# Transposing q and k of the dilated stage by crossbar transfers instead of by TensorE

## The chip, the cores and the metric

The kernel runs on one core of a Trainium2 chip. The metric is the device time of one execution in microseconds (us). A core has a matrix engine (TensorE, PE in the profile, with PEld for its weight loads), a vector engine (DVE), a scalar engine (ACT), GpSimd (POOL) and SyncE (SP), which in this kernel issues most of the transfers; 16 DMA engines carry them. Each engine runs its own instructions strictly in the order in which they stand, and waits on semaphores where it needs another engine's result. SP does the same with the transfers that it issues: a transfer that must wait for its data holds back every transfer behind it.

## The reference

A two-layer encoder over 1024 tokens of width 1024, in float32. Layer 0 mixes tokens by latent attention, layer 1 by dilated sliding-window attention; each layer ends with a squared-ReLU MLP. The change concerns layer 1's mixer alone:

```python
def dilated_mixer(h, pos, w_in, g_q, g_k, rel_bias, w_o):
    proj = (h @ w_in).reshape(B, S, N_DIL_GROUPS, 3, DIL_HEADS, DIL_HEAD_DIM)
    for gi, (window, dilation) in enumerate(DIL_GROUPS):   # (128,1) (512,4) (2048,16)
        q = rms_norm(proj[:, :, gi, 0], g_q[gi])
        k = rms_norm(proj[:, :, gi, 1], g_k[gi])
        v = proj[:, :, gi, 2]
        o, lse = dilated_group(q, k, v, pos, table, window, dilation)
        ...
    # the three groups' outputs are merged by the softmax of their log denominators, then @ w_o
```

There are 16 heads of 64 in each of 3 groups. A query sees 128 keys around it (in the dilated order), with a bias by relative position.

## The kernel before, in words

Products of float32 accuracy are made of float16: a matrix is split into a high half `hi` = f16(x) and a low half `lo` = f16(x - hi), and three matmuls (hi·hi, lo·hi, hi·lo) are summed in PSUM. This is the helper `mm3` (L532 to L534), and `products` (L2345) does the same for the scores. The program holds a second, float32r form of everything (`half` is False), which runs only if a check on the data fails; it does not run here.

The dilated stage is the method `dil`. It takes 3 groups × 8 pairs of heads × 4 token-tile pairs = 96 **steps**; a step is (group g, head pair `pr`, `tp`), where `tp` counts pairs of 128-token tiles. A head pair's four steps form a *unit*. The loop over steps is software pipelined; one pass of the loop emits, in this order:

- `attend` (L2381): for two token tiles whose q and k are ready: 12 score matmuls (`products`, out `pss`), then `scores` (bias and maximum on DVE, L2366; exponentials on ACT, L2372), then the probabilities' halves `ph` (high half on ACT, L2409; low half on DVE and POOL, L2410), then one crossbar transpose issued on SP, `pT<-ph` (L2411).
- The projection of this step's q and k: 48 matmuls of 128×256 into `psproj`, in two halves of 24 (`project`).
- Between the two halves: `stacks` of the step before the last one: four float32 transposes on PE against the identity, `psq<-ident,qn` (L2316), then the split into halves while PSUM is read: high half on ACT (L2321, scaled by 64), low half on DVE (L2322). Both write the tile `kT`, which holds for one unit, in f16, k transposed for all 1024 tokens and **two slots** of q (256 columns each, by `tp % 2`).
- `av` (L2424, L2425): the product with V of the attention emitted one pass earlier, from `pT`.
- `qkstep` of this step's projection: squares on ACT (L2295), sum on DVE (L2296), reciprocal root (ACT L132, L133; DVE L134 to L136), a guard sum on POOL (L2300 to L2302), then `qn` = normalised q and k in the tokens' layout (DVE L2305), and q's gain on POOL (L2307).

So what `qkstep` makes in pass n is transposed in pass n+2 and used by `attend` in pass n+3; an `attend` of pass n is used by `av` in pass n+1. Inside these bounds a scheduler orders each engine's instructions when the program is built.

SP issues for a unit four `wqkr` weight loads (L1968), one bias tile `bt` (L2354), the finished `U` of a unit (L2448 in group 0, two of L2452 in group 1, none in group 2), and for every second unit the V tiles `vraw` (four transfers in group 0, seven in group 1, four in group 2; L2250 to L2266), beside one `pT` for each step. Each transfer takes the next of eight completion semaphores in turn.

Of the kernel before, what the change touches and what calls it, by code (L numbers as in the profile page):

```python
# [20 lines left out]
P = 128  # L21
D = 1024
S = 1024
# [18 lines left out]
class K:  # L42
# [2148 lines left out]
    def dil(self, at0, at1, tail, wqk, vd):  # L2191


        nc, a, tc = self.nc, self.a, self.tc
# [5 lines left out]
        D_ = lambda name, shape, dt, bufs: dpool.tile(list(shape), dt, tag=name, bufs=bufs, name=self.nm(name))  # L2200
# [6 lines left out]
        if self.half:  # L2207
            most = dpool.tile([P, 8], F32, name="most", bufs=1)
            nc.gpsimd.memset(most, 0.0)
            self.nseen += 1  # L2210
            s_ = self.seen[:, self.nseen - 1 : self.nseen]
            nc.vector.tensor_reduce(s_, gain, op=ALU.max, axis=AX.XY, apply_absolute_value=True)
            nc.vector.tensor_scalar(s_, s_, 4.0, None, op0=ALU.mult)
        else:
            nc.vector.tensor_scalar(gain, gain, self.ss, None, op0=ALU.mult)
        stat = dpool.tile([P, 3, 8, 2, H], F32, name="stat", bufs=1)
        Ud = self.DR([8, S, 2, P], "U")
        oTd = self.DR([6, 2, P, 2, 512], "oTd", F16 if self.half else F32)
# [70 lines left out]
        def qkstep(u, tp, ps):  # L2289

            g = u["g"]
            p8 = ps.rearrange("p (n e) -> p n e", e=64)
# [4 lines left out]
            r = self.rstd(ms, 8, "dr", self.half)  # L2297
# [4 lines left out]
                nc.gpsimd.tensor_tensor(most, most, y4, op=ALU.add)  # L2302
            qn = self.T("qn")
            q8 = qn.rearrange("p (n e) -> p n e", e=64)
            nc.vector.tensor_tensor(q8, p8, r.unsqueeze(2).broadcast_to([P, 8, 64]), op=ALU.mult)  # L2305
            qq = qn.rearrange("p (i n e) -> p i n e", i=2, e=64)[:, :, 0:2, :]
            nc.gpsimd.tensor_tensor(qq, qq, gain[:, g : g + 1, :].unsqueeze(1).broadcast_to([P, 2, 2, 64]), op=ALU.mult)  # L2307
            return qn

        def stacks(u, tp, qn):  # L2310

            ps = PS("psq")
            for k in range(2):
                for i in range(2):
                    c = i * 256 + (1 - k) * P
                    nc.tensor.transpose(ps[:, (2 * k + i) * P : (2 * k + i + 1) * P], qn[:, c : c + P], self.ident)  # L2316
            s1 = 4 + tp % 2
            hi, lo = (u["k"][:, k, :].rearrange("p (s x) -> p s x", x=256)[:, tp : s1 + 1 : s1 - tp, :] for k in range(2))
            x = ps.rearrange("p (k x) -> p k x", k=2)
            if self.half:  # L2320
                nc.scalar.activation(hi, x, AF.Copy, scale=64.0)  # L2321
                nc.vector.scalar_tensor_tensor(lo, x, 64.0, hi, op0=ALU.mult, op1=ALU.subtract)  # L2322
            else:
                nc.scalar.activation(hi, x, AF.Copy)
                nc.vector.tensor_tensor(lo, x, hi.bitcast(F32), op=ALU.subtract)
            for i in range(2):
                c = S + (tp % 2 * 2 + i) * P
                u["q"][2 * tp + i] = u["k"][:, :, c : c + P]

        def span(g, t):  # L2330
# [214 lines left out]
        end = max(n for n, x in enumerate(steps) if x is not None)  # L2545
# [75 lines left out]
        for n, step in enumerate(steps):  # L2621
# [271 lines left out]
```

## Time and profile before

| | |
|---|---|
| time, 3 runs | 3007.86 us median (3006.16 to 3011.14) |
| the profiled execution's own time | 3005.26 us |
| its span | 3003.1 us, granted TensorE clock 0.985 |
| busy over the span | PE 94%, DVE 75%, ACT 56%, POOL 31% |
| dilated stage, first to last score matmul | 1552 to 2321 us |
| PE busy in that stage | 710.58 us of 768.5 us |
| largest waits of PE there | on `pT` 25.0 us, on `kT` 14.8 us (DVE's half) and 7.8 us (ACT's half) |

The profile's page gives busy time by engine, 40 equal slices of the span, the transfers by queue, the chain that ended last, and the costliest groups of instructions. A group's row reads: line, engine, operation, output<-input, partitions × elements and type, count, then busy time or durations. In a timeline a row is start (us), duration (us), engine or queue, line, operation; `x2` at the end means that two such instructions in a row were merged, and their duration then runs from the first's start to the last's end, a wait between them included. "SPq" is SP's queue: its duration is the time for which SP was occupied with issuing, not the time of the transfer itself. A wait row reads: who waited, for whose result, total us, times, longest us.

### The profile page before, as it was taken

The numbers are of one execution on the slowest core, as the hardware profiler recorded it, in microseconds if no ns is written. First come the engines' busy times: TensorE is split into PE (matmuls) and PEld (weight loads), VectorE is DVE, ScalarE is ACT, GpSimd is POOL, SyncE is SP. The second block draws the span as 40 slices with busy tenths as digits, with TensorE's granted clock in tenths as the row PEclk, the third lists the DMA queues.
The fourth block names the chain that finished last, engine by engine and source line by source line (L and its number), as shares of the span: only waits on it lengthen the run. The fifth ranks groups of instructions, "written<-read, shape, count | busy, mean of one in ns | idle before, by whom it ended". The sixth has DMA issues, their size and how long they took to land. (4 is left out here: it accounts for less than half of the span.)

```text
span 3003.1 us, 54490 instructions
## 1 busy us (share of the span) xinstructions
PE 2827.4 (94%) x20148; PEld 1676.0 (56%) x20148; DVE 2251.4 (75%) x4902; ACT 1684.2 (56%) x3491; POOL 922.6 (31%) x1276
## 2 busy tenths in 40 slices
PE   6878999999999999999999989998998989999998
PEld 5634566544444444444468878876875434444443
DVE  5687777658988966788768877776886699779565
ACT  4677888825455534533238777775664355555341
POOL 6578888700211000000123344453552002110010
PEclk9999999999999999999999999999999999999999
DMA  6267455425654799546436666565656555457763
GB/s 209 72 169 161 94 117 101 131 84 188 235 188 168 251 278 289 199 159 225 171 116 148 146 139 165 145 128 117 150 129 171 144 191 210 158 186 248 238 196 86
DMA packets 589680, 503.08 MB, mean 168 GB/s; under 512 B 292277, under 2 KB 482018, under 8 KB 589402
## 3 DMA queue, kind: packets, MB, share of 16 engines
q1 hardware_dynamic: 553722, 400.74, 47.9%
q0 software_dynamic: 25248, 87.22, 7.9%
q10 hardware_dynamic: 10432, 11.54, 1.6%
q8 instruction: 159, 2.61, 0.4%
q14 instruction: 119, 0.97, 0.1%
HBM read 317.40 MB, written 125.12 MB: 147 GB/s over the span
## 5 line engine op out<-in xcount | busy, mean ns | idle before, releaser
L534 PE MATMUL psm<-hf,wf 128*128 128x512 f16 x896 | 335.8, 381 | 11.1 <-DVE wf L161 11.1
L532 PE MATMUL psm<-hf,wf 128*128 128x512 f16 x896 | 341.0, 381 | 5.0 <-ACT wf L156 5.0
L533 PE MATMUL psm<-d,d 128*128 128x512 f16 x896 | 340.8, 381 | 4.7 <-DVE d L161 4.7
L534 PE MATMUL psm<-d,d 128*128 128x512 f16 x896 | 340.7, 380 | 0.0
L533 PE MATMUL psm<-hf,wf 128*128 128x512 f16 x896 | 340.6, 380 | 0.0
L532 PE MATMUL psm<-d,d 128*128 128x512 f16 x896 | 335.0, 380 | 0.3 <-ACT d L156 0.3
L1276 POOL TENSOR_TENSOR pp<-p,pp 128x1024 f16<-128x1024 f32 x125 | 275.4, 2209 | 57.9 <-ACT pp L1269 47.8
L532 PE MATMUL psproj<-wqk,hTp 128*128 128x256 f16 x1024 | 283.0, 276 | 0.0
L533 PE MATMUL psproj<-wqk,hTp 128*128 128x256 f16 x1024 | 282.3, 276 | 0.0
L534 PE MATMUL psproj<-wqk,hTp 128*128 128x256 f16 x1024 | 282.0, 275 | 0.0
L156 ACT ACTIVATE d<-ufr 128x1024 f16<-128x1024 f32 x112 | 117.8, 1052 | 211.3 <-PE psm L534 173.3
L897 DVE TENSOR_REDUCE mx<-pmx 128x1 f32<-128x512 f32 x240 | 162.8, 687 | 78.8 <-PE pmx L895 77.4
L161 DVE SCALAR_TENSOR_TENSOR d<-ufr,d 128x1024 f16<-128x1024 f32 x112 | 136.5, 1219 | 76.5 <-ACT d L156 76.4
L1268 ACT ACTIVATE p<-pss 128x512 f32<-128x512 f32 x256 | 149.9, 590 | 43.2 <-PE pss L1259 41.8
L2372 ACT ACTIVATE pd<-pd,dnb 128x192 f32<-128x192 f32 (+2 forms) x384 | 167.3, 437 | 4.1 <-POOL y L2301 2.3
L534 PEld LDWEIGHTS <-wf 128*128 128x128 f16 x896 | 87.8, 98 | 123.3 <-DVE wf L161 19.2
L532 PEld LDWEIGHTS <-wf 128*128 128x128 f16 x896 | 87.9, 98 | 112.9 <-ACT wf L156 10.9
L534 PEld LDWEIGHTS <-d 128*128 128x128 f16 x896 | 87.9, 98 | 111.0 <-issue 6.4
L532 PEld LDWEIGHTS <-d 128*128 128x128 f16 x896 | 88.0, 98 | 106.3 <-issue 2.2
L533 PEld LDWEIGHTS <-d 128*128 128x128 f16 x896 | 87.9, 98 | 106.4 <-issue 2.5
L2410 POOL TENSOR_TENSOR ph<-pd,ph 128x512 f16<-128x512 f32 (+1 forms) x121 | 113.3, 942 | 109.3 <-ACT ph L2409 109.1
L533 PEld LDWEIGHTS <-wf 128*128 128x128 f16 x896 | 88.0, 98 | 104.9 <-issue 1.8
(439 smaller groups left out, 8122.2 us busy)
## 6 DMA issues: line engine op xcount, KB each, us to landing
ufr<-uf SPq DMA_DIRECT2D x112, 512.0 KB
w2r<-in_mlp_w SPq DMA_DIRECT2D x96, 512.0 KB
adaw<-in_ada_w SPq DMA_DIRECT2D x80, 512.0 KB
w1r<-in_mlp_w SPq DMA_DIRECT2D x64, 512.0 KB
wqkr<-in_dil_w_in SPq DMA_DIRECT2D x96, 256.0 KB
wvr<-in_dil_w_in SPq DMA_DIRECT2D x34, 512.0 KB
uf<-ub POOLq DMA_DIRECT2D x32, 512.0 KB, 3.8
uf<-ua POOLq DMA_DIRECT2D x32, 512.0 KB, 3.3
```

The source lines that it names most:

```text
L156: nc.scalar.activation(hi, src, AF.Copy, scale=scale)
L161: return nc.vector.scalar_tensor_tensor(lo, src, scale, hi, op0=ALU.mult, op1=ALU.subtract, accum_out=self.seen[:, self.nseen - 1 : self.n ...
L532: mm(out, lh, rh, start=first, stop=False)
L533: mm(out, lh, rl, start=False, stop=False)
L534: mm(out, ll, rh, start=False, stop=last)
L897: nc.vector.tensor_reduce(maxes[h][:, 2 * j + b : 2 * j + b + 1], ps, op=ALU.max, axis=AX.X)
L1268: nc.scalar.activation(p[:, b * 512 : (b + 1) * 512], ps[b], AF.Exp, scale=1.0 / self.ss)
L1276: eng.tensor_tensor(q[:, 1], p, q[:, 0], op=ALU.subtract)
L2372: nc.scalar.activation(p[:, e, lo:hi], p[:, e, lo:hi], AF.Exp, scale=1.0 / self.ss, bias=nb[:, e : e + 1], accum_out=stat[:, g, t, 1, 2 * ...
L2410: (nc.gpsimd if i or u["g"] == 2 else nc.vector).tensor_tensor(lo, p, hi, op=ALU.subtract)
```

## The change

In the f16 form, q and k are no longer transposed by PE and split out of PSUM. `qkstep`'s last DVE instruction now also multiplies by 64. A new function `qkturn`, called one pass after `qkstep` (so one pass earlier than the transposes of before), splits `qn` in the tokens' layout into a float16 tile `hl`: high half on ACT, low half on POOL, each 128×512. Then four crossbar transposes on SP (`dma_start_transpose`) put `hl`'s high k, high q, low k and low q, each 128 tokens × 256 columns, transposed into `kT`. `kT` has three slots for q instead of two. `stacks` then has nothing to do for these steps and only hands the slots on; the last two of the 96 steps still go by PE.

```diff
+        NQ = 3 if self.half else 2
...
-            nc.vector.tensor_tensor(q8, p8, r.unsqueeze(2).broadcast_to([P, 8, 64]), op=ALU.mult)
+            rb = r.unsqueeze(2).broadcast_to([P, 8, 64])
+            if self.half:
+                nc.vector.scalar_tensor_tensor(q8, p8, 64.0, rb, op0=ALU.mult, op1=ALU.mult)
+            else:
+                nc.vector.tensor_tensor(q8, p8, rb, op=ALU.mult)
...
+        def qkturn(u, tp, qn):
+
+            hl = D_("hl", (P, 2, 2, 2, P), F16, 2)
+            x = qn.rearrange("p (i s c) -> p s i c", i=2, s=2)
+            nc.scalar.activation(hl[:, 0], x, AF.Copy)
+            nc.gpsimd.tensor_tensor(hl[:, 1], x, hl[:, 0], op=ALU.subtract)
+            for k in range(2):
+                for s, c in ((1, tp * 256), (0, S + tp % NQ * 256)):
+                    nc.sync.dma_start_transpose(out=u["k"][:, k, c : c + 256].rearrange("p (i c) -> p i c", c=P),
+                                                in_=hl[:, k, s].rearrange("p i c -> p (i c)"))
+            for i in range(2):
+                c = S + (tp % NQ * 2 + i) * P
+                u["q"][2 * tp + i] = u["k"][:, :, c : c + P]
+
         def stacks(u, tp, qn):
 
+            if qn is None:
+                return
             ps = PS("psq")
...
-            if self.half:
-                nc.scalar.activation(hi, x, AF.Copy, scale=64.0)
-                nc.vector.scalar_tensor_tensor(lo, x, 64.0, hi, op0=ALU.mult, op1=ALU.subtract)
-            else:
-                nc.scalar.activation(hi, x, AF.Copy)
-                nc.vector.tensor_tensor(lo, x, hi.bitcast(F32), op=ALU.subtract)
+            nc.scalar.activation(hi, x, AF.Copy)
+            nc.vector.tensor_tensor(lo, x, hi if self.half else hi.bitcast(F32), op=ALU.subtract)
...
-                                      "k": D_("kT", (P, 2, S + 512), self.DT, 2), "U": self.G("U", (P, 8, P), F32)}
+                                      "k": D_("kT", (P, 2, S + 256 * NQ), self.DT, 2), "U": self.G("U", (P, 8, P), F32)}
...
+            if self.half and stacking is not None and n < end:
+                qkturn(*stacking)
+                stacking = stacking[:2] + (None,)
             stk.append(stacking)
```

How the instructions move. On PE, at the middle of one step's projection in group 1 (`hTp` is the permuted input's half, `wqk` the weights), there stood before:

```order
L533 MATMUL psproj_22794<-wqk_22612,hTp_20623 128x256
L534 LDWEIGHTS hTp_20623
L534 MATMUL psproj_22794<-wqk_22612,hTp_20623 128x256
L2316 MATMUL psq_22819<-ident,qn_22603 128x128 x4
L532 LDWEIGHTS hTp_20201
L532 MATMUL psproj_22794<-wqk_22609,hTp_20201 128x256
```

and there stands now:

```order
L533 MATMUL psproj_22801<-wqk_22619,hTp_20630 128x256
L534 LDWEIGHTS hTp_20630
L534 MATMUL psproj_22801<-wqk_22619,hTp_20630 128x256
L532 LDWEIGHTS hTp_20208
L532 MATMUL psproj_22801<-wqk_22616,hTp_20208 128x256
```

The four transposes are gone and the two halves of the projection follow each other; the rest of PE's order in a step is as it was.

On SP, late in group 1, over two units with a set of V loads; before:

```order
L2354 DMA bt_23873<-bias_138 128x2x256
L2411 DMA_TRANSPOSE pT_23185<-ph_23184 128x16x128
L2452 DMA U<-U_22198 512x1x128
L2411 DMA_TRANSPOSE pT_23335<-ph_23334 128x16x128
L2452 DMA U<-U_22198 512x1x128
L1968 DMA wqkr_23492<-in_dil_w_in 128x4x128 x2
L2411 DMA_TRANSPOSE pT_23470<-ph_23469 128x16x128
L2411 DMA_TRANSPOSE pT_23607<-ph_23606 128x16x128
L1968 DMA wqkr_23771<-in_dil_w_in 128x4x128 x2
```

and now, at the same place:

```order
L2428 DMA_TRANSPOSE pT_23342<-ph_23341 128x16x128
L1968 DMA wqkr_23214<-in_dil_w_in 128x4x128
L2323 DMA_TRANSPOSE kT_22759<-hl_23390 128x2x128 x4
L2469 DMA U<-U_22205 512x1x128 x2
L2428 DMA_TRANSPOSE pT_23477<-ph_23476 128x16x128
L1968 DMA wqkr_23499<-in_dil_w_in 128x4x128
L2323 DMA_TRANSPOSE kT_23323<-hl_23526 128x2x128 x4
L2428 DMA_TRANSPOSE pT_23614<-ph_23613 128x16x128
L1968 DMA wqkr_23499<-in_dil_w_in 128x4x128
L2323 DMA_TRANSPOSE kT_23323<-hl_23662 128x2x128 x4
L1968 DMA wqkr_23778<-in_dil_w_in 128x4x128
```

From one `pT` (128×16×128) to the next there now stand, nearly everywhere, four `kT` transposes of 128×2×128 (L2323) in the same queue.

On POOL, two steps' pieces of the same group; now:

```order
L2312 TENSOR_TENSOR qn_22610<-qn_22610,dgain 128x2x128
L2427 TENSOR_TENSOR ph_22636<-pd_22648,ph_22636 128x512
L2320 TENSOR_TENSOR hl_22686<-qn_22610,hl_22686 128x512
L2393 MEMSET pd_22789 128x2x64
L2395 MEMSET pd_22917 128x2x64
L2301 TENSOR_TENSOR y_3627_22749<-dry_22741 128x8
L2302 TENSOR_TENSOR y_3627_22749<-y_3627_22749 128x8
L2303 TENSOR_TENSOR most<-most,y_3627_22749 128x8
L2312 TENSOR_TENSOR qn_22753<-qn_22753,dgain 128x2x128
L2427 TENSOR_TENSOR ph_22777<-pd_22789,ph_22777 128x512
L2320 TENSOR_TENSOR hl_22826<-qn_22753,hl_22826 128x512
```

`hl`'s low half (L2320) is new; it stands mostly behind the low half of `ph` (L2427, L2410 before), which `pT` waits for. Otherwise POOL's order is that of before. On ACT `hl`'s high half (L2319) stands about where `kT<-psq` (L2321) stood.

More of the change, by code (lines that the diff above doesn't have):

```diff
@@ L2316, in stacks @@
                     nc.tensor.transpose(ps[:, (2 * k + i) * P : (2 * k + i + 1) * P], qn[:, c : c + P], self.ident)
-            s1 = 4 + tp % 2
+            s1 = 4 + tp % NQ
             hi, lo = (u["k"][:, k, :].rearrange("p (s x) -> p s x", x=256)[:, tp : s1 + 1 : s1 - tp, :] for k in range(2))
             x = ps.rearrange("p (k x) -> p k x", k=2)
-            if self.half:
-                nc.scalar.activation(hi, x, AF.Copy, scale=64.0)
-                nc.vector.scalar_tensor_tensor(lo, x, 64.0, hi, op0=ALU.mult, op1=ALU.subtract)
-            else:
-                nc.scalar.activation(hi, x, AF.Copy)
-                nc.vector.tensor_tensor(lo, x, hi.bitcast(F32), op=ALU.subtract)
+            nc.scalar.activation(hi, x, AF.Copy)
+            nc.vector.tensor_tensor(lo, x, hi if self.half else hi.bitcast(F32), op=ALU.subtract)
             for i in range(2):
-                c = S + (tp % 2 * 2 + i) * P
+                c = S + (tp % NQ * 2 + i) * P
                 u["q"][2 * tp + i] = u["k"][:, :, c : c + P]
```

## The prediction

> **What bounds the kernel now.** I read the windows of the dilated stage first (columns: stretch, its length, then busy us and instructions of PE, PEld, DVE, ACT, POOL, the clock, the DMA share and GB/s): stretches of group 0, group 1 and group 2.
>
> ```profile
> 1552.00:1726.00 174.00, 172.92 (x1894) 150.57 (x1894) 140.70 (x452) 137.52 (x405) 66.88 (x134) 1.00 0.59 138
> 1794.80:1975.60 180.80, 174.16 (x1926) 152.04 (x1924) 136.62 (x467) 136.09 (x415) 73.05 (x174) 1.00 0.63 151
> 2118.50:2241.90 123.40, 114.99 (x1189) 99.57 (x1188) 107.40 (x353) 82.64 (x285) 66.31 (x113) 1.00 0.64 141
> ```
>
> PE is busy for 99%, 96% and 93% of them, no other engine above 87%: inside a group PE sets the pace. The timeline gives its step, in group 1 and in group 2, from one step's score matmuls to the next:
>
> ```profile
> 1900.54 0.83 PE L2345 MATMUL pss<-kT 64*128 64x256 f16 x12
> ...
> 1903.93 0.60 PE L2316 MATMUL psq<-ident,qn 128*128 128x128 f32 x4
> 1904.36 0.27 PE L532 MATMUL psproj<-wqk,hTp 128*128 128x256 f16 x1
> ...
> 1907.76 0.83 PE L2345 MATMUL pss<-kT 64*128 64x256 f16 x12
> ...
> 2197.22 0.83 PE L2345 MATMUL pss<-kT 64*128 64x256 f16 x12
> ...
> 2204.10 0.83 PE L2345 MATMUL pss<-kT 64*128 64x256 f16 x12
> ```
>
> A step takes 7.22 us, in group 2 6.88; the four transposes hold PE from 1903.93 to 1904.36, 0.43 us. What PE waits for, over the stage:
>
> ```profile
> PE psav L2424 <- DMA pT<-ph: 25.0, 12, 6.2
> PE pss L2345 <- DVE kT L2322: 14.8, 12, 2.8
> PE pss L2345 <- ACT kT L2321: 7.8, 10, 1.8
> ```
>
> Last I read SP's queue, since the change adds there. Two units of group 1, from the `pT` after one set of V loads to the `pT` after the next:
>
> ```profile
> 1864.94 3.83 SPq L2411 DMA_TRANSPOSE pT<-ph  x1
> 1868.86 0.56 SPq L2452 DMA_DIRECT2D U<-U  x1
> 1870.32 1.53 SPq L2411 DMA_TRANSPOSE pT<-ph  x1
> 1871.94 0.55 SPq L2452 DMA_DIRECT2D U<-U  x1
> 1872.54 1.25 SPq L1968 DMA_DIRECT2D wqkr<-in_dil_w_in  x2
> ...
> 1907.72 9.43 SPq L2411 DMA_TRANSPOSE pT<-ph  x2
> 1917.19 0.58 SPq L1968 DMA_DIRECT2D wqkr<-in_dil_w_in  x1
> ...
> 1923.73 0.44 SPq L2354 DMA_DIRECT2D bt<-bias  x1
> 1924.34 4.02 SPq L2411 DMA_TRANSPOSE pT<-ph  x1
> ```
>
> These 8 steps take 1924.34 - 1864.94 = 59.4 us. The rows of the kinds (ns: shortest, median, longest):
>
> ```profile
> L2411 SPq DMA_TRANSPOSE pT<-ph x93: 1232/1599/4400, 1559.2 to 2290.4; - x93
> L1968 SPq DMA_DIRECT2D wqkr<-in_dil_w_in x96: 368/577/2099, 1446.1 to 2229.7; - x96
> L2452 SPq DMA_DIRECT2D U<-U x16: 534/558/608, 1835.3 to 2071.7; - x16
> L2259 SPq DMA_DIRECT2D vraw<-v x8: 582/599/1329, 1730.7 to 1921.1; - x8
> L2354 SPq DMA_DIRECT2D bt<-bias x24: 366/444/1525, 1506.6 to 2206.2; - x24
> L2266 SPq DMA_DIRECT2D vraw<-v x16: 609/616/1355, 1978.5 to 2183.8; - x16
> ```
>
> Eight `pT` (3.83 for the one behind the V loads, 7 at 1.60: 15.0), eight `wqkr` (4.6), four `U` (2.2), seven `vraw` (4.2) and two `bt` (0.9) keep SP issuing for 26.9 us of the 59.4. The rest it spends waiting, for the most part on `ph`; none of it is on PE's path today except where `pT` comes late.
>
> **The change part by part.** *Removed from PE:* 94 of 96 steps lose 0.43 us. PE alone would then need 6.79 us a step in groups 0 and 1 and 6.45 in group 2.
>
> *Removed from DVE, exchanged on ACT, added on POOL.*
>
> ```profile
> L2321 ACT ACTIVATE kT<-psq x96: 569/574/598, 1549.6 to 2317.2; 128x512 f16<-128x512 f32 x96
> L2322 DVE SCALAR_TENSOR_TENSOR kT<-psq,kT x96: 671/688/693, 1550.2 to 2318.8; 128x512 f16<-128x512 f32 x96
> ...
> L2409 ACT ACTIVATE ph<-pd x186: 398/614/632, 1557.4 to 2283.6; 128x512 f16<-128x512 f32 x128, 128x256 f16<-128x256 f32 x58
> ...
> L2410 POOL TENSOR_TENSOR ph<-pd,ph x121: 663/1152/1607, 1565.1 to 2289.7; 128x512 f16<-128x512 f32 x63, 128x256 f16<-128x256 f32 x58
> ```
>
> DVE loses 0.69 us a step; the factor of 64 costs nothing, since `qn` stays one pass over the same 128×512. ACT gives 0.57 for 0.61 us. POOL gains a subtraction of the same shapes as L2410's large form, 1.15 us a step: in group 1's window it rises from 73 to about 102 of 181 us. It hides beside PE's step; without that cover it would cost up to 94 × 1.15 = 108 us. I cost these three at nothing. With the eviction its waits on PE's path, 14.8 + 7.8 us, go too; the same matmuls now wait for the transfers, so I do not book them as a gain.
>
> *Added on SP:* 376 transposes of 128×2×128, 4 a step. No row shows one this small. From below, the ordinary transfers of this queue take 0.37 to 0.62 us; from above, a `pT` of 8 blocks (those of group 2) takes at least 1.23, and one cannot well cost more than a transfer of four times its size. Between the sizes:
>
> ```profile
> 1870.32 1.53 SPq L2411 DMA_TRANSPOSE pT<-ph  x1
> ```
>
> is a `pT` of 16 blocks that met nothing. Half the blocks save only 0.30 us, 0.037 a block, so a fixed 0.93 us stands before any block, and 2 blocks come to 1.01. The median of all `pT` lies above these undisturbed ones, so I take **1.05 us**, near the transposes' rows and far from the ordinary transfers', and keep 0.55 and 1.25 as ends. [...]
>
> For two units, SP then issues for 26.9 + 32 × 1.05 = 60.5 us. That is above PE's 8 × 6.79 = 54.3 and above today's 59.4: **in groups 0 and 1 SP takes PE's place as the bound**, 1.1 us worse for 8 steps, so for 64 steps +9. Group 0 has fewer `U` and V loads but the same transposes; I leave it in. In group 2, eight `pT` at 1.23, eight `wqkr`, four `vraw` at 0.62 and two `bt` make 17.9, with the new ones 51.5, against PE's 8 × 6.45 = 51.6: PE stays the bound, and about half of its 32 steps, those at 6.88, give back 0.43: -7.
>
> *The queue's order.* A `pT` can now stand behind up to four `kT` (4.2 us), and a `kT` behind a `pT` that waits for its `ph`. In the step above, POOL ends the `ph` half late:
>
> ```profile
> 1906.54 1.16 POOL L2410 TENSOR_TENSOR ph<-pd,ph 128x512 f16<-128x512 f32 x1 [1.81 <-ACT ph L2409]
> ```
>
> so SP took `pT` at 1907.72; `hl`'s low half follows on POOL and is ready near 1908.9. SP would issue the high pair from about 1906.5, `pT`, then the low pair, and be through near 1912.3, for score matmuls two steps after 1900.54, at 1914.9 or, at PE's new pace, 1914.1: the slack is about 2 us. Behind a set of V loads (4.2 us, and the `pT` behind it 3.83 in place of 1.6) it is gone, and what is late next is `kT` before L2345 and `pT` before L2424, both on PE. There are 12 such sets; today they already stretch a step, and part of it is in the sum for SP. I add +6 for the rest, from nothing to 2 us a set.
>
> *DMA engines.* In these 59.4 us:
>
> ```profile
> DMA packets 24658, 9.02 MB, mean 152 GB/s; under 512 B 16976, under 2 KB 24649, under 8 KB 24649
> ...
> q1 hardware_dynamic: 24649, 8.91, 62.3%
> ```
>
> Most packets are the transposes' 256 bytes; 32 × 64 KB add 8192, a third, so the share rises to at most about 83%: covered, at the price of queueing that is in the +6. The group changes and the stage's end, with steps of 10 to 17 us, have SP to spare: 0.
>
> *Sum:* 3005.26 + 9 - 7 + 6 = 3013. The profiled run lies 2.6 us under the median of the runs shown, so I forecast a median of **3016 us**.
>
> **The rivals.** *A, small transposes issue like ordinary transfers,* 0.55 us: two units need 26.9 + 17.6 = 44.5 on SP, PE stays the bound everywhere and gives back 0.43 us in some 64 steps that it fills, 28, and a few of the 22.6 us of waits on `kT`: 2977. For it: `U`, also 128 partitions out of SBUF, takes 0.56. Against: no transpose in the trace is under 1.16, those of the first layer included:
>
> ```profile
> L842 SPq DMA_TRANSPOSE q<-qkv x32: 1165/1334/2529, 194.4 to 527.2; - x32
> ```
>
> [...]
>
> *B, a stream of transposes pays for the one before it:* 1.25 us each, from the point where two stand back to back. Then two units need 66.9, 7.5 more than today: over the 8 pairs of units in groups 0 and 1 +60, group 2 with 17.9 + 40 = 57.9 still under today's pace: 3066, slower. For it: `pT` reaches 4.40 behind other transfers. Against: those follow V loads, not small transposes.
>
> *C, it comes out even:* 1.0 us and no queueing, SP at 58.9 for 59.4, group 2's gain against the V loads' loss: within the noise of 3008.
>
> *D, POOL:* if `hl`'s subtraction mostly went ahead of `ph`'s, `pT` would be 1.15 later in each step; the order shows it mostly behind. With it some 30 steps lose 0.5: 3030.
>
> **How the numbers follow.** A measurement here tells 0.2%, 6 us, from no change. The forecast case (0.97 to 1.15 us an issue) has 0.42: its span reaches from 3000 to 3040, so faster 0.06, same 0.10, slower 0.26. A 0.27, faster. B 0.18, slower. C 0.08: same 0.05, faster 0.03. D 0.05, slower. Together: **faster 0.36, same 0.15, slower 0.49**. The range takes in A's 2977 with a little for the waits on `kT`, and B's 3066: 2968 to 3068; the forecast's own is 3000 to 3040.
>
> **What would show it.** Right: SPq rows of `kT<-hl` near 1.0 us; SP issuing nearly without a gap in groups 0 and 1; score matmuls or `av` waiting on DMA `kT` and `pT` for some 50 us; steps of about 7.4 us there and near 6.5 in group 2; DVE 65 us less. Wrong: `kT<-hl` near 0.55 us and steps of 6.79 (A), or PE waiting while SP stands idle, which would put the loss on POOL or on landing times.

## The result and the profile after

The changed kernel takes **3160.69 us** (median of 4 runs, 3156.54 to 3162.84) against 3007.01 us for the kernel before on the same chip (3005.58 to 3011.14): a ratio of **1.0516**, interval 1.0502 to 1.053. That is 154 us slower, where 9 us were forecast, and far outside the range, which ended at 3068.

The page of the changed kernel, its first part (busy us, share, instructions):

```profile
PE 2864.4 (91%) x19772; PEld 1661.8 (53%) x19772; DVE 2221.5 (70%) x4808; ACT 1693.4 (54%) x3491; POOL 1028.7 (33%) x1370
```

PE issues 376 matmuls fewer and is busy 37 us *longer* than before (2827.4): the transposes are gone, but other matmuls take more time each (those of `psproj`, 128×256, start 0.21 us apart at 1628 us, where the granted clock is 0.50, and 0.11 apart at 1621 us, where it is 1.00). All of the loss lies in the dilated stage. Its windows, columns as in the prediction's first fence:

```profile
1552.00:1726.00 174.00, 144.46 (x1432) 115.58 (x1429) 105.64 (x344) 112.19 (x324) 78.58 (x132) 0.92 0.63 142
1900.00:2100.00 200.00, 163.32 (x1623) 130.00 (x1622) 113.15 (x389) 124.90 (x374) 86.42 (x173) 0.91 0.63 143
2100.00:2300.00 200.00, 154.00 (x1415) 121.83 (x1413) 122.78 (x409) 111.81 (x364) 104.34 (x166) 0.83 0.73 142
```

PE was busy for 99% of the first window and is now busy for 83%, and the granted clock, 1.00 before, is 0.92, 0.91 and 0.83. From the first to the last score matmul the stage takes 928 us instead of 769. What PE waits for there (us in total, times, longest):

```profile
PE pss L2362 <- DMA kT<-hl: 102.9, 90, 4.0
PE psav L2441 <- DMA pT<-ph: 57.5, 28, 4.3
```

As foreseen, the score matmuls wait for `kT` and `av` for `pT`, 160 us together instead of 48. And SP's queue, from one `pT` to the ninth, which is the prediction's stretch of 8 steps with the same contents (8 `pT`, 8 `wqkr`, 4 `U`, 7 `vraw`, 2 `bt`, and now 32 `kT`; its middle is left out):

```profile
1912.65 2.47 SPq L2428 DMA_TRANSPOSE pT<-ph  x1
1915.23 5.07 SPq L2323 DMA_TRANSPOSE kT<-hl  x4
1920.35 1.27 SPq L2469 DMA_DIRECT2D U<-U  x2
1921.80 3.85 SPq L2428 DMA_TRANSPOSE pT<-ph  x1
1925.71 0.57 SPq L1968 DMA_DIRECT2D wqkr<-in_dil_w_in  x1
1926.38 5.04 SPq L2323 DMA_TRANSPOSE kT<-hl  x4
1931.59 1.60 SPq L2428 DMA_TRANSPOSE pT<-ph  x1
...
1982.01 2.56 SPq L2428 DMA_TRANSPOSE pT<-ph  x1
1984.62 4.66 SPq L2323 DMA_TRANSPOSE kT<-hl  x3
1989.44 1.62 SPq L2428 DMA_TRANSPOSE pT<-ph  x1
```

The queue has hardly a gap: of 1989.44 - 1912.65 = 76.8 us it issues for 71.8. A step is 9.6 us long here because SP needs that long for it. The stretch is one of the dearest: over the 64 steps from the first `pT` to the 65th, groups 0 and 1, the kernel before takes 505.5 us and the changed one 606.9, so 101 us more; from there to the last `pT`, 28 steps of group 2, 225.7 becomes 279.5, 54 us more. The rows of the two kinds (ns: shortest, median, longest):

```profile
L2323 SPq DMA_TRANSPOSE kT<-hl x376: 1167/1243/2759, 1550.2 to 2440.5; - x188
L2428 SPq DMA_TRANSPOSE pT<-ph x93: 1231/1597/5042, 1564.4 to 2450.8; - x93
```

### The profile page after: what moved, and what is told of

Read it like the earlier page. It is cut to its first block, busy times and chain, and to the rows that moved or that the text cites. A ratio compares the mean times of both kernels' runs of the same rounds, so it can differ in the third digit from the quotient of the medians.

```text
span 3160.7 us, 54462 instructions
## 1 busy us (share of the span) xinstructions
PE 2864.4 (91%) x19772; PEld 1661.8 (53%) x19772; DVE 2221.5 (70%) x4808; ACT 1693.4 (54%) x3491; POOL 1028.7 (33%) x1370
## 5 line engine op out<-in xcount | busy, mean ns | idle before, releaser
L532 PE MATMUL psproj<-wqk,hTp 128*128 128x256 f16 x1024 | 298.9, 292 | 0.0
L533 PE MATMUL psproj<-wqk,hTp 128*128 128x256 f16 x1024 | 297.5, 290 | 0.0
L534 PE MATMUL psproj<-wqk,hTp 128*128 128x256 f16 x1024 | 296.8, 290 | 0.0
L2362 PE MATMUL pss<-kT 64*128 64x256 f16 x1152 | 109.6, 303 | 112.1 <-DMA kT<-hl 102.9
L2449 DVE TENSOR_REDUCE U<-psav 128x128 f32<-128x256 f32 x192 | 76.3, 420 | 154.5 <-PE psav L2442 154.1
L2383 DVE CUSTOM_DVE_ANT_0 pd<-pss,bt 128x192 f32<-128x192 f32 (+2 forms) x384 | 114.3, 347 | 71.7 <-PE pss L2362 62.6
L534 PEld LDWEIGHTS <-wf 128*128 128x128 f16 x896 | 87.8, 98 | 119.3 <-DVE wf L161 14.8
L532 PEld LDWEIGHTS <-wf 128*128 128x128 f16 x896 | 87.9, 98 | 113.5 <-ACT wf L156 10.6
L271 DVE SCALAR_TENSOR_TENSOR adacc<-adaw,cond,adacc 128x1024 f32<-128x1024 f32 (+1 forms) x98 | 126.4, 1290 | 28.1 <-DMA adaw<-in_ada_w 27.2
L534 PEld LDWEIGHTS <-d 128*128 128x128 f16 x896 | 87.7, 98 | 110.5 <-issue 5.6
```

Of the source, the lines that this page charges most:

```text
L271: return self.nc.vector.scalar_tensor_tensor(acc, w, c, acc, op0=ALU.mult, op1=ALU.add)
L532: mm(out, lh, rh, start=first, stop=False)
L533: mm(out, lh, rl, start=False, stop=False)
L534: mm(out, ll, rh, start=False, stop=last)
L2362: nc.tensor.matmul(pss[e][:, i * 256 : (i + 1) * 256], q[r, a, :], u["k"][r, b, w0 : w0 + 256], start=n == 0, stop=n == 2)
L2383: nc.vector.tensor_tensor_reduce(p[:, e, lo:hi], pss[e][:, i * 256 + lo - off : i * 256 + hi - off], bt[:, e, lo - b0 : hi - b0], op0=ALU. ...
```

## The experiments

Below, "+" gives the difference of a kernel's median from the kernel before on its own chip. Ratios have their 95% intervals.

### Is it SP's issuing, or the reader?

**dummy4**: the kernel before, with TensorE's transposes kept and read, and as many small transposes added as the change has, which nobody reads (in `stacks`, behind the split).

```diff
+            if self.half:
+                for k in range(2):
+                    for c in (tp * 256, S + tp % 2 * 256):
+                        x = D_("dump", (P, 2, P), F16, 8)
+                        nc.sync.dma_start_transpose(out=x, in_=u["k"][:, k, c : c + 256])
```

> The kernel before, with its four transposes on PE and its evictions, plus four crossbar transposes of 128x2x128 a step, out of kT into a scratch tile that nothing reads: 384 issues on SP as in the change, but no engine waits for their data, and DVE, ACT and POOL work as before. Theory (SP's issue time, 1.24 us each, is the bound): SP needs 27 + 32 x 1.24 = 67 us for 8 steps that took 59, PE waits on pT alone: 3090 to 3170 us. Rival 'latency' (the change lost because the score matmuls now wait for a longer chain of hl, issue and landing): nothing waits here, so 3000 to 3020 us.

Measured: 3135.13 us, ratio 1.0417 (1.04 to 1.0435), **+129**. The row of the added transposes:

```profile
L2330 SPq DMA_TRANSPOSE dump<-kT x384: 1167/1240/2997, 1550.8 to 2457.1; - x192
```

PE's largest wait in the stage:

```profile
PE psav L2429 <- DMA pT<-ph: 113.6, 49, 7.3
```

The same 1.24 us each, and PE now waits mostly on `pT`, which stands behind them in SP's order: its wait rises from 25.0 to 113.6 us. The queue itself shows it: summed over the 63 `pT` of groups 0 and 1 behind the first, the time from the end of the last instruction that makes `ph` to SP's taking the `pT` is 10 us in the kernel before, 142 in the changed kernel and 274 in dummy4. The added transposes by themselves, issues and bytes together, cost 129 us, more than four fifths of the loss, although nothing uses what they bring.

**sizes**: the kernel before, with one unread transpose a step, of 1, 2, 4 or 8 blocks of 128×128 by `tp`.

```diff
+            old = units.get((u["g"], u["pr"] - 1))
+            if self.half and old is not None:
+                m = 1 << tp
+                x = D_("dump", (P, 8, P), F16, 2)
+                nc.sync.dma_start_transpose(out=x[:, 0:m], in_=old["k"][:, 0, 0 : m * P])
```

> The kernel before plus one unread transpose a step, of 1, 2, 4 and 8 blocks in turn, out of an older kT. It prices an issue by size on a queue that isn't full. Theory now: a floor of about 1.17 to 1.24 us from 1 to 8 blocks. The prediction's line: 0.97, 1.01, 1.08, 1.23 us. Time: SP has 37 us of work in 59, so 3005 to 3020 us by both.

Measured: 3009.17 us, ratio 1.0003 (0.9993 to 1.0012): no change. All 84 in one row:

```profile
L2330 SPq DMA_TRANSPOSE dump<-kT x84: 1119/1225/2134, 1549.5 to 2266.2; - x84
```

Sorted by size (21 each) the medians are 1.12, 1.24, 1.21 and 1.23 us for 1, 2, 4 and 8 blocks. The price in this run is a floor that hardly depends on the size up to 8 blocks, not the prediction's 0.93 us + 0.037 a block. And one more issue a step cost nothing here, in a queue with room: by the 26.9 us of the kernel before and this row's median an estimated 26.9 + 8 × 1.23 = 37 us of issue in 59.

**burst1**: dummy4's four transposes, but in the steps `tp == 1` alone: about as many as in sizes, bunched by four.

```diff
-            if self.half:
+            if self.half and tp == 1:
```

> The kernel before plus four unread 128x2x128 transposes in the steps tp = 1 alone (96 in all, nearly as many as the 84 that cost nothing when each step had one), so that the number is held and only their bunching changes. Theory Q (four in a row hold SyncE's queue for 5 us at one place, more than the 2 us that the p transpose behind them has to spare): about the 40 us of the quarter-dose kernel plus the 10 us of TensorE time that one saved and this one doesn't: 3030 to 3055. Theory R (what costs is the wait of the score matmuls for k and q on their longer way): nobody reads these, so 3004 to 3013.

Measured: 3001.64 us, ratio 0.999 (0.998 to 1.0): no loss, and theory Q fails for this dose. These transposes, too, bring data made just before (the split of the same step writes what they read). Here a bunch of four was absorbed, in a queue that by the same count issues for an estimated 37 of 59 us:

```profile
L2330 SPq DMA_TRANSPOSE dump<-kT x96: 1168/1240/2445, 1557.6 to 2293.0; - x96
```

### Fewer issues, fewer bytes, another queue

**move**: the changed kernel, with the stage's weight, bias and V loads issued by ACT.

```diff
-            dma = nc.sync.dma_start
+            dma = (nc.scalar if self.half else nc.sync).dma_start
...
-                loads[n] = self.dil_weights(g, pr, parts=parts)
+                loads[n] = self.dil_weights(g, pr, eng=nc.scalar if self.half else None, parts=parts)
```

> The changed kernel with the dilated stage's weight, bias and V loads issued by ACT instead of SP; all transposes stay on SP. About 1.2 us a step leave SP, none of the bytes leave the DMA engines, and ACT gains that much. Theory (SP's issue time): the stage's 96 steps lose up to 1.2 us each: 3040 to 3090 us. Rival 'DMA engines' (the added 25 MB of 256-byte packets are the bound) and rival 'latency': 3145 to 3175 us.

Measured: 3138.82 us, ratio 1.0443 (1.0425 to 1.046), +132. Taking 1.2 us a step away from SP's queue gives back only 22 us, less than the theory forecast, more than its rivals. It isn't free on the other side either: ACT now spends some 87 us issuing these loads. SP issues for 704 us of a stage of 906 (summed from its rows), so it was no longer quite full, and the waits on `kT` (96.3 us) and `pT` (67.6 us) stayed: room alone, at this fill and at this price on ACT, doesn't bring the time back.

**pair**: the changed kernel, with the q and k of two steps in one set of four transposes of 128×4×128 (four slots for q, attention one pass later): the same bytes, half the issues.

```diff
-            hl = D_("hl", (P, 2, 2, 2, P), F16, 2)
+            j = tp % 2
+            if j == 0:
+                u["hl"] = D_("hl", (P, 2, 2, 4, P), F16, 2)
+            hl = u["hl"]
...
+            if j == 0:
+                return
...
-                for s, c in ((1, tp * 256), (0, S + tp % NQ * 256)):
+                for s, c in ((1, (tp - 1) * 256), (0, S + (tp - 1) * 256)):
```

> The changed kernel with q and k of two steps split into one tile and transposed together: four transposes of 128x4x128 for two steps, so half the issues for the same bytes; kT has four slots for q, and a step's attention comes one pass later. Theory (issue time by count): SP needs 27 + 16 x 1.25 = 47 us for 8 steps, PE is the bound again at 6.79 us a step: 2965 to 3000 us, under the kernel before. Rival 'DMA engines': the bytes are the same, 3140 to 3170 us. Rival 'latency': the pass more gives slack, but the even step's data wait for the odd one's: 3000 to 3100 us.

Measured: 3084.8 us, ratio 1.0241 (1.0217 to 1.0264), +78. Half the issues, half the loss; SP issues for 579 of 848 us. The theory's 2965 to 3000 is missed, and the time lies in the range given to the rival of latency; the later pass, which pair has as well, is priced by itself under lag below, at some 12 us of the 76. The DMA engines, at a faster pace, are fuller than in any other kernel here (share 0.80 and 0.84, second last column):

```profile
1557.00:1750.00 193.00, 171.06 (x1760) 141.01 (x1758) 129.45 (x425) 133.48 (x393) 92.18 (x157) 0.95 0.80 164
1834.00:2030.00 196.00, 172.82 (x1833) 143.95 (x1832) 123.27 (x441) 138.77 (x420) 99.01 (x198) 0.97 0.84 171
```

**smallw** and **pair_smallw**: the changed kernel, and pair, with the bytes of the weight loads cut to a quarter and the number of transfers kept. They load one quarter of the weight matrix of q and k and use it four times, so they leave out three quarters of it and their results are others.

```diff
+            if self.half and parts is not None:
+                c0 = (g * 3 + k) * 1024 + 2 * pr * 64
+                self.nc.sync.dma_start(out=raws[half][:, 0, k * P : (k + 1) * P], in_=w_in[half * 512 : half * 512 + P, c0 : c0 + P])
+                return
...
-                self.parts(hi, lo, raw, self.ws)
+                self.parts(hi, lo, raw[:, 0:1].broadcast_to([P, 4, 256]) if self.half and parts is not None else raw, self.ws)
```

> The changed kernel with the same number of transfers, but the loads of the dilated stage's q/k weights bring a quarter of their bytes (one 128-row piece, used four times in place of the four pieces, so the q and k of that stage are computed with a weight matrix that repeats one quarter). Theory S (SyncE's stream, counted in instructions): nothing changes, 3145 to 3170. Theory B (the 16 DMA engines' load, whose busy share was 0.63 to 0.74 in the stage, delays the transposes): the bytes that go out are most of what the stage loads, and 3060 to 3110 would be seen.

> The kernel in which two steps' q and k share four transposes (3084.8, half the small issues, the same transposed bytes, DMA engines busy 0.75 to 0.84 of the stage), with the same cut of the weight loads to a quarter of their bytes (the weights of q and k of the dilated stage repeat one quarter of the matrix). Theory S or order on SyncE's queue: 3070 to 3090, no change. Theory B: with the DMA share brought under its value before the change (about 0.6) the remaining loss of 78 us shrinks to 10 to 30 us, 3015 to 3040.

Measured: smallw 3145.85 us, ratio 1.0457 (1.044 to 1.0474), +140; pair_smallw 3058.31 us, ratio 1.0172 (1.0155 to 1.0189), +52. In the changed kernel the bytes carry about 14 of 154 us; in pair, where the share falls from 0.84 to 0.74, 26 of 78:

```profile
1834.00:2030.00 196.00, 180.83 (x1936) 151.62 (x1933) 132.24 (x463) 146.41 (x436) 107.30 (x213) 0.97 0.74 157
```

So theory S holds for the change against B, and theory B is a lesser part that shows once the queue has room. Neither expectation for pair_smallw was met; it came out between them.

**acthi** and **pair_acthi**: the high halves' transposes issued by ACT, those of the low halves by SP; the second on top of pair.

```diff
-                    nc.sync.dma_start_transpose(out=u["k"][:, k, c : c + 256].rearrange("p (i c) -> p i c", c=P),
+                    (nc.sync if k else nc.scalar).dma_start_transpose(out=u["k"][:, k, c : c + 256].rearrange("p (i c) -> p i c", c=P),
```

> The changed kernel with the two transposes of the high halves issued by ScalarE, right behind the copy that makes them, and the two of the low halves by SyncE: same transfers, two queues. Theory Q: SyncE's bunch shrinks from 5 to 2.5 us and its issue in 8 steps from 68 to 47 us; ScalarE, busy 54%, takes 2.5 us more per step of 7 us: 3030 to 3090. If what bounds is the way of the halves (copy, subtraction, landing) or the DMA engines, nothing is gained: 3130 to 3165.

> Both at once: two steps share four transposes (3084.8 with all on SyncE) and the high halves' two are issued by ScalarE. SyncE then has one small issue per step as in the kernel with one unread transpose per step, which cost nothing. Theory Q: 2985 to 3025, on the side of the kernel before or better, since TensorE no longer does its four transposes. Theory B (the DMA engines' load, which gave back 26 of 78 us when bytes were cut): 3045 to 3085.

Measured: acthi 3599.03 us, ratio 1.1969 (1.1949 to 1.1989), +594; pair_acthi 3347.24 us, ratio 1.1142 (1.1124 to 1.1161), +342. No theory had this. SP's largest own waits in acthi, in the first 780 us of a stage of 1368 us:

```profile
SPq L2323 <- DMA kT<-hl: 267.5, 64, 12.2
SPq L2428 <- DMA kT<-hl: 147.2, 42, 5.4
```

and a piece of the two queues' timelines:

```profile
1681.26 11.21 ACTq L2323 DMA_TRANSPOSE kT<-hl  x2
...
1681.58 0.59 SPq L1968 DMA_DIRECT2D wqkr<-in_dil_w_in  x1
1688.96 1.18 SPq L2323 DMA_TRANSPOSE kT<-hl  x1
1693.73 1.63 SPq L2428 DMA_TRANSPOSE pT<-ph  x1
```

Each queue's transposes wait for the landing of the other's: SP for 415 us here and for 726 over the whole stage, and ACT, whose two transposes of some 1.18 us each stretch over 11.21 us, computes nothing meanwhile (it stands idle for 11.10 us). By the semaphores' records ACT's first one lands at 1688.91, and SP's next transpose goes at 1688.96; that lands at 1691.27, and ACT's second goes at 1691.29; that lands at 1693.58, and `pT` goes at 1693.73. Over the stage none of ACT's 188 transposes is in flight together with one of SP's 281, while in the changed kernel, with one queue, 424 of the 469 start before the one ahead of them has landed. The turns of the eight completion semaphores aren't the reason: the one that SP's transpose of 1688.96 takes had been free since 1679.74, and the ordinary `wqkr` load goes out between without a wait. In this program, then, transposes of two queues go strictly one after the other, and under that order a second queue doesn't carry the load.

**hlv**: the changed kernel, with the low half computed on DVE instead of POOL.

```diff
-            nc.gpsimd.tensor_tensor(hl[:, 1], x, hl[:, 0], op=ALU.subtract)
+            nc.vector.tensor_tensor(hl[:, 1], x, hl[:, 0], op=ALU.subtract)
```

> The changed kernel with the low half of q and k computed on VectorE (0.69 us for such a subtraction) instead of GpSimd (1.16 us, in order behind the gain and ahead of the low half of p): rival D of the prediction. Theory Q: the queue behind it is as full as before, 3140 to 3170. Theory D (GpSimd is late): 3060 to 3120.

Measured: 3165.11 us, ratio 1.0535 (1.0518 to 1.0553), +160: no gain. DVE has part of `ph`'s low halves in its own order, so the subtraction has moved in front of other work rather than away; but POOL's part of it isn't what decides at full dose.

### The dose

**dose1** and **dose2**: the changed kernel, with the crossbar used in the steps `tp == 1` alone, or 1 and 3; the others go through TensorE.

```diff
-            if self.half and stacking is not None and n < end:
+            if self.half and stacking is not None and n < end and stacking[1] in (1,):
```

> One part of the change alone, in a quarter of the places: only the step tp = 1 of each unit sends its q and k through the crossbar (about 94 small transposes in the kernel instead of 376), the other three quarters go through TensorE as before. Theory S (SyncE's instruction stream is what runs out; it issued 27 us in a stretch of 8 steps of 59.4 us before, and 66 to 75 us of 70 to 81 us in the changed kernel): 27 + 8 x 1.24 = 37 us of 59, far from full, so nothing is lost, and the TensorE transposes that fall away, 0.43 us in 23 steps, are worth up to 10 us: 2997 to 3012. Theory T (each step that takes this way costs a fixed sum, its landing and the clock after it: 154 us / 92 steps = 1.7 us): 3007 + 23 x 1.7 = 3046.

> The same in half of the places (the steps tp = 1 and tp = 3 of each unit, about 188 small transposes). Theory S: 27 + 16 x 1.24 = 47 us of issue in 59 us, near four fifths; a queue that is not full but that has the p transposes waiting in order behind the small ones: 3005 to 3040, well under half of the loss of 154 us. Theory T: 3007 + 46 x 1.7 = 3085, half of the loss.

Measured: dose1 3047.28 us, ratio 1.0123 (1.0099 to 1.0148), +41; dose2 3056.79 us, ratio 1.0161 (1.0144 to 1.0178), +51. The first quarter of the dose costs 41 us, the second 10, the last half 103. Theory T meets dose1 and misses dose2. Theory S explains the last half, not the first quarter, where SP issues for 442 of 814 us only. As burst1 showed, the issues by themselves aren't to blame there either: dose1 has as many, 96. What dose1 adds to them is the making of the halves, and that what they bring is read.

**lag1**, **lag2** and **lag**: dose1, dose2 and the changed kernel, with the attention one pass later, so that k and q have a pass of 7 us more.

```diff
-        NQ = 3 if self.half else 2
+        NQ = 4 if self.half else 2
...
                 if x is not None:
                     stacks(*x)
+                lag.append(x)
+                x = lag.pop(0) if len(lag) > self.half else None
+                if x is not None:
                     u_, tp_ = x[:2]
```

> The quarter dose (tp = 1 through the crossbar, the rest by TensorE), with the attention of every step moved one pass later (a fourth slot for q, one more empty pass at the end), so that k and q have one pass of about 7 us more. Theory R: the 40 us go and TensorE's 10 us are kept: 2990 to 3010. Theory H: 3035 to 3050, as without the pass.

> The same with the steps tp = 1 and 3 (half dose, 3056.8 without the extra pass). SyncE then issues about 47 us in a stretch of 59. Theory R: 2985 to 3020. Theory H or a queue that is already too full at four fifths: 3040 to 3065.

> The changed kernel, all steps, with the extra pass. The queue is full whatever the slack of the reader: with 26.9 + 32 x 1.27 = 67.5 us of issue in 8 steps instead of the 59.4 of the kernel before, 3090 to 3140; if the reader's wait (R) were all of the loss: 2975 to 3010; if nothing of it (H and the queue): 3150 to 3165.

Measured: lag1 3043.6 us, ratio 1.0139 (1.0117 to 1.0161), +39; lag2 3044.43 us, ratio 1.0121 (1.0094 to 1.0147), +40; lag 3147.16 us, ratio 1.0468 (1.045 to 1.0485), +142. In lag no wait on `kT` is left in the list, yet the time stays. The wait has only moved:

```profile
PE psav L2441 <- DMA pT<-ph: 146.9, 54, 7.0
```

So the 102.9 us that the score matmuls wait for `kT` in the changed kernel were not a term of their own; they are where a full queue happened to show. Against the 154 of the full dose, the reader's slack is worth some 12 us (no run has the later pass alone on the kernel before); lag came out between its expectations. At the small dose theory R fails altogether: 2 us.

**hd1**: the kernel before, with the halves made and transposed in the steps `tp == 1`, unread. **hl1**: the same without the transposes (without the loop below). **hl4**: hl1 in all steps.

```diff
+            hl = D_("hl", (P, 2, 2, 2, P), F16, 2)
+            x = qn.rearrange("p (i s c) -> p s i c", i=2, s=2)
+            nc.scalar.activation(hl[:, 0], x, AF.Copy, scale=64.0)
+            nc.gpsimd.tensor_tensor(hl[:, 1], x, hl[:, 0], op=ALU.subtract)
+            for k in range(2):
+                for s in range(2):
+                    x = D_("dump", (P, 2, P), F16, 8)
+                    nc.sync.dma_start_transpose(out=x, in_=hl[:, k, s].rearrange("p i c -> p (i c)"))
```

> The kernel before, TensorE's transposes kept and read, plus in the steps tp = 1 the halves of the change (ScalarE's copy, GpSimd's subtraction) and their four transposes, which nobody reads. Theory H (the transposes wait on SyncE for their halves, and the p transpose behind them waits along): 3035 to 3055, as the quarter dose with 10 us of TensorE time more. Theory R (only a reader of k and q loses, because their way has become longer than the pass): 3003 to 3014.

> The kernel before, with TensorE's transposes kept and read, plus ScalarE's copy and GpSimd's subtraction of the halves in the steps tp = 1, which nobody transposes or reads: no instruction of SyncE is added. Theory H (SyncE's order): 3002 to 3010, no change. Theory E (the two stand in front of p's own copy and subtraction, 0.6 + 1.2 us, where p has little to spare): 3030 to 3050, as hd1.

> The same in all steps of the stage. Theory H: at most 15 us for GpSimd's and ScalarE's 1.8 us per step, 3003 to 3020. Theory E: at least twice what a quarter of the steps costs, 3070 to 3160, which would make the halves by themselves as dear as the full queue (129 us), with the two lying beside each other in the changed kernel.

Measured: hd1 3047.27 us, ratio 1.0141 (1.0124 to 1.0157), **+42**; hl1 3022.33 us, ratio 1.0052 (1.0035 to 1.0069), **+15**; hl4 3040.82 us, ratio 1.0103 (1.008 to 1.0125), **+34**. hd1 costs what dose1 costs, unread, though it keeps TensorE's 10 us: a reader accounts for no more than that. hl1 shows that a part of it is the making of the halves, which the prediction had costed at nothing; hl1 and hl4 both came out between their two expectations. hd1's timeline, on ACT, POOL and SP, at such a step:

```profile
1679.29 0.62 ACT L2314 ACTIVATE hl<-qn 128x512 f16<-128x512 f32 x1
1679.81 0.61 ACT L2420 ACTIVATE ph<-pd 128x512 f16<-128x512 f32 x1
...
1679.93 2.46 SPq L2319 DMA_TRANSPOSE dump<-hl  x2
...
1679.99 1.16 POOL L2315 TENSOR_TENSOR hl<-qn,hl 128x512 f16<-128x512 f32 x1 [1.99 <-ACT hl L2314]
...
1681.10 1.15 POOL L2421 TENSOR_TENSOR ph<-pd,ph 128x512 f16<-128x512 f32 x1
...
1682.55 3.03 SPq L2422 DMA_TRANSPOSE pT<-ph  x1
```

On both engines `hl` stands in front of `ph`, and `pT` goes out 2.13 us after ACT's copy of `ph` ends (1680.42). The kernel before, at the same place:

```profile
1680.91 0.62 ACT L2409 ACTIVATE ph<-pd 128x512 f16<-128x512 f32 x1
...
1681.60 1.16 POOL L2410 TENSOR_TENSOR ph<-pd,ph 128x512 f16<-128x512 f32 x1 [1.93 <-ACT ph L2409]
...
1682.78 1.73 SPq L2411 DMA_TRANSPOSE pT<-ph  x1
```

Nothing stands between, and it is 1.25 us. That is the prediction's rival D, in the steps that it thought few. They aren't few: in the changed kernel a `ph` follows directly on `hl` in POOL's order in 36 of 94 steps, in 28 of them without a gap, and `hl` directly on `ph` in 39, so the front part's "mostly behind" is wrong.

How much of hl4's 34 us the changed kernel pays is not shown. hl4 keeps TensorE's way, and there the halves also stand in front of that way's own copies. PE's waits in hl4:

```profile
PE psav L2431 <- DMA pT<-ph: 31.6, 18, 5.0
PE pss L2352 <- DVE kT L2329: 30.8, 19, 3.7
```

Against 25.0 and 14.8 before, the larger growth is on `kT` from DVE, a wait that the changed kernel no longer has.

The remaining 27 us of hd1 belong neither to the halves alone (+15) nor to the transposes alone (burst1, -4), but to the two together. A suspect is SP's order: a small transpose stands at the queue's head, not yet allowed to go, with `pT` behind it. SP's longest waits of hd1 (us, times, longest):

```profile
SPq L2319 <- ACT dsq L2295: 96.7, 16, 14.4
SPq L2422 <- DVE ph L2421: 63.0, 24, 7.5
```

(The releaser named, `dsq`, is an ACT instruction that follows `hl` and `ph`; the transposes go 0.02 us after `hl` is made.) But that wait is for `hl`'s high half, and where `hl` stands in front of `ph`, the `pT` behind isn't ready yet either. Counted as under dummy4, over 63 `pT` of groups 0 and 1, a finished `ph` stood 38 us before SP took it in hd1, and 32 in burst1, which lost nothing. What differs is `pT`'s own issue: all 93 take 162 us in the kernel before, 171 in burst1, 171 in hl1 and 200 in hd1, and PE's wait on `pT` goes with it, 25.0, 19.8, 30.2 and 47.5 us. Why the issue grows isn't settled, so the cause of the 27 us stays open.

No kernel that reads what the crossbar brings beat the kernel before: the best that the dose experiments allow is TensorE's 0.43 us in a quarter of the steps, 10 us, and the halves cost 15 there.

## Why the prediction was wrong

The mechanism was named: SP takes PE's place as the bound in groups 0 and 1. The size was off in nearly every term, and group 2 was put on the wrong side. The stretch of 8 steps shows the terms, since the prediction worked out the same one:

| 8 steps on SP, us | predicted | measured |
|---|---|---|
| 32 `kT` | 33.6 (1.05 each) | 41.0 (1.28 each) |
| 8 `pT` | 15.0 | 19.0 |
| `wqkr`, `U`, `vraw`, `bt` | 11.9 | 11.8 |
| gaps | 0 | 5.0 |
| sum | 60.5 | 76.8 |

- **"I take 1.05 us" an issue: wrong, the first step that failed.** The line through 16 and 8 blocks was drawn out to 2 blocks, where the cost is flat: 1.24 us median, 1.28 mean in this stretch. Rival B's 1.25 was the right price, and for the wrong reason: one transpose alone costs the same (1.24 us for 2 blocks in sizes). The prediction had the row that says so (`x32: 1165/1334/2529`, with 1.16 as the least of all transposes) and used it only against rival A. Rival A's 0.55 us, taken from the ordinary transfers, is less than half of the shortest transpose that a row of these runs shows, 1.12 us (sizes). In pair, half the issues for the same bytes, with the later pass, gave back 76 of 154 us.
- **The right price alone gives less than half of the loss.** 26.9 + 32 × 1.28 = 67.9 us instead of 59.4 is +68 for groups 0 and 1, where 101 were measured. The rest of it stands in the table's second and fourth lines. In group 2 the price gives 17.9 + 41.0 = 58.9, still under the 61.5 to 64.5 us that the kernel before really takes there for 8 steps.
- **"Queue order +6": wrong.** It was treated as an accident of the 12 sets of V loads. With the queue full it is not an accident of these sets: in this stretch the `pT`, 1.88 us each on the prediction's count, take 2.37, and 5.0 us pass in gaps, and over groups 0 and 1 a finished `ph` stands 142 us instead of 10 before its `pT` is taken. Why `pT`'s own issue grows is not settled.
- **"Group 2: PE stays the bound, -7": wrong, by the second failed step.** It took one step of 6.88 us for the pace, but the kernel before takes 61.5 to 64.5 us for 8 there, 7.7 or more each, with PE busy for 219 of 250 us, so PE alone didn't set that pace. Measured is +54 us, a third of the loss, with the lowest PE share of the three windows (77%) and clock (0.83). In two stretches of 8 steps SP issues for 59.2 of 74.1 us and 58.2 of 73.2, so it isn't full, and PE waits 41.6 us on `kT` and 19.3 on `pT`. dummy4 loses 35 us in the same steps with unread transposes. What makes up the rest is open.
- **"DVE, ACT, POOL at nothing": wrong by up to 34 us** (hl4, whose PE waits grow more on TensorE's way than on `pT`). The work was hidden by PE's step in its sum, 102 of 181 us on POOL, but not in its place: in over a third of the steps it stands in front of `ph`, which `pT` waits for. Rival D had the mechanism, with some 30 such steps, at 0.05 and 3030. What of it is left beside the full queue isn't shown (hlv has no gain).
- **"PE loses 0.43 us a step": right but worthless.** A rough sorting of the spacing of the stage's matmul starts, into full-speed spacing, what the half clock adds to it, and gaps, gives some 610, 10 and 150 us before, 565, 60 and 300 after: about 45 us less to do, 50 us more for stretched matmuls, 150 us more of gaps.
- **A slower clock after stalls: not in the prediction at all.** The 50 us of stretched matmuls come with 218 us of the stage at half the granted clock, instead of 31 (summed from the clock's records). The last section shows it.
- **"DMA engines covered, at most 83%": held.** The share is 0.63 to 0.73 at the slower pace; smallw's 14 us are its price here.

The parts measured apart don't add up: unread transposes 129, halves at most 34, reader some 12, less up to 40 that TensorE is spared, make 135 of 154, and they overlap. hd1 shows at a quarter of the dose that halves and transposes together cost more than each apart; that this is the rest at full dose is not shown.

## What to carry to other kernels

Before moving work from an engine to a queue, count what that queue issues in the tightest stretch, at the price of the shortest instruction of the kind that the trace has, not at a line drawn below it; a queue served in order can delay what stands in it well before 100%: in pair, with SP issuing for 68% of its stage, PE waited 58.7 us on `pT` (25.0 before), and the kernel still lost 78 us, though not by the queue alone. Take the pace that the price is compared with from many steps, not from one. Work that looks hidden by its sum has to be followed to its place in each engine's order: hl1 put 0.6 and 1.2 us into a quarter of the steps, on engines that were busy for 56% and 31%, and lost 15 us. An unread copy of the added transfers, or of the added arithmetic, is a cheap way to price each by itself.

## What the runs showed of the hardware

**The issue of a crossbar transpose on SP was nearly flat up to 8 blocks:** medians of 1.12 to 1.24 us for 1 to 8 blocks of 128×128 in f16 (sizes), 1.53 for an undisturbed one of 16 (the kernel before, at 1870.32).

**Behind short stalls PE's granted clock was halved for longer than they lasted**, 6.8 us at 0.50 behind a wait of 1.62. Four windows of the changed kernel, about one place; the third last column is the granted clock:

```profile
1620.00:1625.10 5.10, 3.03 (x40) 2.25 (x37) 1.63 (x4) 2.73 (x7) 2.26 (x2) 1.00 0.47 104
1625.10:1631.90 6.80, 4.65 (x24) 2.88 (x25) 3.91 (x17) 4.41 (x15) 3.43 (x6) 0.50 0.67 155
1632.00:1652.00 20.00, 17.12 (x183) 14.52 (x181) 12.16 (x36) 13.68 (x39) 8.81 (x15) 1.00 0.66 165
1652.50:1662.60 10.10, 8.38 (x53) 5.53 (x54) 4.66 (x17) 4.22 (x13) 3.18 (x7) 0.50 0.73 159
```

and the stall ahead of the first halved stretch:

```profile
1623.30 0.23 PE L2441 MATMUL psav<-vs,pT 128*128 128x128 f16 x1 [1.62 <-DMA pT<-ph]
```

PE was busy for 3.03 of the first 5.1 us, and the next 6.8 us ran at 0.50: a wait of 1.62 us and a few small ones stood ahead, with PE busy for 39% of the last 3.41 us. The clock's records agree over the whole stage: it has 31 stretches at half clock, nearly all of 3.41, 6.83 or 10.24 us, and in the 3.41 us ahead of each PE was busy for at most 49%, which only 7% of the equally long windows at full clock fall below. PE gets through 183 matmuls in the 20 us of the third window, at full clock, and through 53 in the 10.1 us of the fourth, at half; not all of that is the clock, since it waits there too. PE's longest wait on a transfer in the stage is 4.3 us; in the 3.41 us ahead of 10 of the 31 stretches it stands idle for less than 2 us at a time.

**One queue kept several transposes in flight, two that took turns did not:** in the changed kernel 424 of 469 start before the one ahead of them has landed (median 2.7 us from issue to landing); in acthi, where the program orders the two queues' transposes one behind the other, SP waits 726 us for landings, at +594 us in all.
